# Splitting weights into high and low parts: the two parts side by side in one buffer, and moving tiles 288 floats apart

## The chip, the cores and the metric

One core of one Trainium2 chip runs the whole program. The metric is the device time of one execution in microseconds (us); for several executions the median is given. TensorE is called PE in the rows, its weight loads PEld; DVE is VectorE, ACT is ScalarE, POOL is GpSimd, SP is SyncE.

## What is computed

One inference step of a two-layer decoder trunk, on 256 prompt tokens and 8 sampled tokens at once (264 columns). Cut to what matters:

```python
for l in range(2):
    p = rmsnorm(h, norm1_g[l]) @ w_in[l]          # 2048 -> 5120
    a, bg, cg, hh, q, k, v, g, u, vv = split(p, 10)
    mix = concat(pool_mixer(a), conv_mixer(bg, cg, hh), retention(q, k, v, g), sgu_mixer(u, vv))
    h = h + mix @ w_out[l]                         # 2048 -> 2048
    gt, up = split(rmsnorm(h, norm2_g[l]) @ w_gate_up[l], 2)   # 2048 -> 2 x 5632
    h = h + (silu(gt) * up) @ w_down[l]            # 5632 -> 2048
y = rmsnorm(h, final_norm_g)
```

All inputs are float32 and the result has to be close to a float32 product. The mixers are small beside the four large products.

## The kernel before, in words

Activations lie transposed: 128 channels on the partitions, the 264 tokens along the free dimension. Every large product is made of 128x128 weight blocks. TensorE takes them in a reduced float32 form (`F32R`), so each operand is split in two: a high part, which is the value rounded to that form, and a low part, which is the remainder. A product of a weight block and a moving tile is then three matmuls into the same PSUM bank, in the function `work`:

```python
mm(ps, wl, xh[:], c["left"] == c["nk"], False)   # low weights,  high activations
mm(ps, wh, xl[:], False, False)                  # high weights, low activations
mm(ps, wh, xh[:], False, c["left"] == 0)         # high weights, high activations
```

Each of them is one weight load of 128 columns and one matmul with 264 moving columns; the weight load of the next matmul runs while the present one streams.

Weights come from HBM by DMA from SP's queue into `raw` (seven buffers, each of 8 blocks of 128x128, 512 KB). `do_split` (line 270 and the helper at line 120) turns a `raw` buffer into a high buffer `whi` with a cast on ScalarE and into a low buffer `wlo` with a subtraction on VectorE. There are four buffers of each kind (`NH = 4`). In them a block is 128 floats in a row per partition, and the high and the low buffer lie 16 KB apart. Weight buffers are split up to four ahead of the matmuls that read them, and loaded up to seven ahead of the split; waits between engines are semaphores. One buffer of 8 blocks feeds 24 matmuls.

The moving tiles are `XH[k]` and `XL[k]` (high and low part of the normalised input, 16 each) for the input and the gate/up product, and tiles `r` from a pool of 33 for the output and the down product. They lie next to each other, 264 floats (1,056 bytes) apart on each partition. Matmuls of the large products are written out in the rows as `acc<-xh,wlo`, `acc<-xl,whi`, `acc<-xh,whi`, `acc<-r,wlo` and `acc<-r,whi`. They all go through the helper `mm` at line 117. The small matmuls of the mixers go into `ms` banks, most of them in plain float32: such a matmul stands in the trace as two records.

Phases follow each other per layer: `in` (40 output chunks of 16 blocks), `out` (16 chunks of 16), then three groups of `gu` (32, 32 and 24 chunks of 16) and `dn` (16 chunks of 16, 16 and 12 blocks). In the `in` phase the generators in `tasks` (pooling, retention, gated unit) put their small matmuls between the chunks. For the retention of the sampled tokens, a constant `sel` of 8 blocks of 128 columns picks one token and spreads it over the partitions.

Of the kernel before, what the change touches and what calls it, by code (L numbers as in the profile page):

```python
# [11 lines left out]
F32R = mybir.dt.float32r  # L12
I32 = mybir.dt.int32
AF = mybir.ActivationFunctionType
ALU = mybir.AluOpType
AX = mybir.AxisListType

P = 128
L = 2
D = 2048  # L20
KD = D // P
NP = 256
NS = 8
T = NP + NS
# [8 lines left out]
SUB = 8  # L33
NH = 4
NR = 7
NT = 20
NRR = 33
TW = 272
TB = 88
VL = 32  # L40

# [10 lines left out]
def hybrid_step(ctx, tc, I, O):  # L52
    nc = tc.nc
    pe, ve, se, po, sy = nc.tensor, nc.vector, nc.scalar, nc.gpsimd, nc.sync
# [4 lines left out]
    def mk(name, shape, dt=F32):  # L59
        return sb.tile(shape, dt, tag=name, name=name)  # L60

    H4 = [mk(f"h{i}", [P, 4, T]) for i in range(4)]
    h = [H4[k // 4][:, k % 4, :] for k in range(KD)]
    XH = [mk(f"xh{k}", [P, T], F32R) for k in range(KD)]
    XL = [mk(f"xl{k}", [P, T], F32R) for k in range(KD)]
    raw = [mk(f"raw{i}", [P, SUB, P]) for i in range(NR)]
    whi = [mk(f"whi{i}", [P, SUB, P], F32R) for i in range(NH)]
    wlo = [mk(f"wlo{i}", [P, SUB, P], F32R) for i in range(NH)]
    rfree = deque(mk(f"r{i}", [P, T], F32R) for i in range(NRR))
    tfree = deque(mk(f"t{i}", [P, TW]) for i in range(NT))  # L70
    acc = [pp.tile([P, 512], F32, tag=f"acc{i}", name=f"acc{i}") for i in range(4)]
    misc = deque(pp.tile([P, 512], F32, tag=f"ms{i}", name=f"ms{i}") for i in range(4))
# [6 lines left out]
    ccol = mk("ccol", [P, 6 + 4 * 16 + KD])  # L79
    kdec, rcnt = ccol[:, 0:4], ccol[:, 6:70].rearrange("p (g t) -> p g t", g=4)  # L80
    mean128, mean2048, gfin = ccol[:, 4:5], ccol[:, 5:6], ccol[:, 70:70 + KD]
    sel = mk("sel", [VL + NS, NS, P], F32R)

    cols = mk("cols", [P, NC_COL])
    sgrow = mk("sgrow", [P, GW])
# [9 lines left out]
    vhl = mk("vhl", [VL + NS, GW], F32R)  # L95
# [8 lines left out]
    def ta():  # L104
        return tfree.popleft()

    def tf(*ts):
        tfree.extend(ts)

    def ma():  # L110
        return misc.popleft()

    def mf(*ts):
        misc.extend(ts)

    def mm(out, lhsT, rhs, start=True, stop=True):
        pe.matmul(out, lhsT, rhs, start=start, stop=stop)  # L117

    def tt(out, a, b, op, eng=None):
        (eng or ve).tensor_tensor(out=out, in0=a, in1=b, op=op)  # L120

    def stt(out, a, s, b, op0, op1):
        ve.scalar_tensor_tensor(out=out, in0=a, scalar=s, in1=b, op0=op0, op1=op1)  # L123

    def ts(out, a, s1, s2, op0, op1, eng=None):
        if s2 is None:
            (eng or ve).tensor_scalar(out=out, in0=a, scalar1=s1, scalar2=None, op0=op0)
        else:
            (eng or ve).tensor_scalar(out=out, in0=a, scalar1=s1, scalar2=s2, op0=op0, op1=op1)

    def scaled(out, a, s):
        se.activation(out, a, AF.Identity, scale=s)  # L132

    def f(ap):
        return ap.bitcast(F32)
# [8 lines left out]

    def split(src):
        hi, lo = rfree.popleft(), rfree.popleft()
        se.copy(hi[:], src)  # L147
        tt(lo[:], src, f(hi[:]), ALU.subtract)
        return hi, lo

    def split_ps(src, s):
        hi, lo = rfree.popleft(), rfree.popleft()
        scaled(hi[:], src, s)
        stt(lo[:], src, s, f(hi[:]), ALU.mult, ALU.subtract)
        return hi, lo

    def token_rsqrt(srcs, wcol):
        n = len(srcs)
        ps = ma()
        for c in range(3):  # L160
            cc = slice(c * TB, (c + 1) * TB)
            for i, parts in enumerate(srcs):
                for x, part in enumerate(parts):
                    mm(ps[:TB, c * n + i:c * n + i + 1], part[:, cc], wcol, x == 0, x == len(parts) - 1)
        w = 3 * n
        m, t, r = (small[:TB, q, :w] for q in range(3))
        ts(m, ps[:TB, :w], EPS, None, ALU.add, None)
        mf(ps)
# [3 lines left out]
    def token_bcast(ps, r, i, n):  # L172
        for c in range(3):
            mm(ps[:, c * TB:(c + 1) * TB], r[:, c * n + i:c * n + i + 1].to_broadcast([TB, P]), ident[:TB, :TB])

# [31 lines left out]
            return (r, ps) if both else r  # L207

    def to_x(k, gcol):
        scaled(XH[k][:], h[k], gcol)  # L210
        stt(XL[k][:], h[k], gcol, f(XH[k][:]), ALU.mult, ALU.subtract)

    subs = []
    phases = []
# [68 lines left out]
    def work(c, k0, k1, xs):  # L283
        if c["ps"] is None:
            c["ps"] = accfree.popleft()
        ps = c["ps"][:, :T]
        for k in range(k0, k1):
            j = c["subs"][k // SUB]
            if k == k0 or k % SUB == 0:
                do_split(j + NH)  # L290
                assert state["split"] > j
            wh, wl = whi[j % NH][:, k % SUB, :], wlo[j % NH][:, k % SUB, :]
            xh, xl = xs[k]
            mm(ps, wl, xh[:], c["left"] == c["nk"], False)
            mm(ps, wh, xl[:], False, False)
            c["left"] -= 1
            subs[j]["left"] -= 1
            mm(ps, wh, xh[:], False, c["left"] == 0)

    def run(cs, xs, evac, stats=None, bcast=None, hooks=None, defer=2):  # L300
        nk = cs[0]["nk"]
# [59 lines left out]
    def in_phase(l, cs, rms, hooks=None):  # L361
# [22 lines left out]
        def evac(c):  # L384
# [15 lines left out]
            elif grp == O_VV:  # L400
                vvT[j] = ta()
                tt(vvT[j][:, :T], ps[:, :T], r[:, :T], ALU.mult)
                if j == 0:
                    tasks.append(ret_sample())
# [50 lines left out]
        def pool(j, e):  # L455
            win = WINDOWS[j]
            s, w = e, 1
            while w < win:
                o = ta()
                lo = 2 * w - 1  # L460
                tt(o[:, lo:TW], s[:, lo:TW], s[:, lo - w:TW - w], ALU.add)
                if s is not e:
                    tf(s)
                s, w = o, 2 * w
            d, t = ta(), ta()
            stt(d[:, :NP], s[:, 16:TW], 1.0 / win, e[:, 16:TW], ALU.mult, ALU.subtract)
            tt(t[:, 0:16], s[:, 16:32], rcnt[:, j, :], ALU.mult)
            tt(d[:, 0:16], t[:, 0:16], e[:, 16:32], ALU.subtract)
            ve.tensor_reduce(out=t[:, 16:24], in_=exts[:, j, :, 16 - win:16], axis=AX.X, op=ALU.add)
            stt(d[:, NP:T], t[:, 16:24], 1.0 / win, exts[:, j, :, 15], ALU.mult, ALU.subtract)  # L470
            po.tensor_copy(pouts[:, j, :], e[:, TW - 15:TW])
            tf(s, e, t)
# [50 lines left out]
        def ret_sample():  # L523
            yield
            yield
            yield
            ob = None
            for b in range(NS + 1):
                if b > 0:
                    if ob is None:  # L530
                        ob = ma()
                    S = sst[(b - 1) % 3]
                    for j in range(4):
                        mm(ob[:, j * NS + b - 1:j * NS + b], S[:, j, :], qs[:, j, b - 1:b])
                    po.dma_start(out=O["ret_s"][l, :, b - 1], in_=S[:])
                    if b + 2 < NS:
                        sy.dma_start(out=S[:], in_=I["s_ret"][l, :, b + 2])
                if b < NS:
                    S = sst[b % 3]
                    vb = ma()  # L540
                    mm(vb[:], sel[:, b, :], vhl[:])
                    for j in range(4):
                        se.mul(S[:, j, :], S[:, j, :], GAMMA[j])
                        stt(S[:, j, :], vb[:, j * P:(j + 1) * P], ks[:, j, b:b + 1], S[:, j, :], ALU.mult, ALU.add)
                    mf(vb)
                yield
            for j in range(4):
                se.copy(oT[j][:, NP:T], ob[:, j * NS:(j + 1) * NS])
            mf(ob)
# [67 lines left out]

        run(cs, list(zip(XH, XL)), evac, rms.stats, bcast, hooks)
        assert not tasks
# [15 lines left out]
    def gu_phase(cs, rms, r2):  # L635
# [22 lines left out]
        if rms is None:  # L658
            run(cs, list(zip(XH, XL)), evac)
        else:  # L660
            run(cs, list(zip(XH, XL)), evac, rms.stats, bcast)
        return act, X["r"]
# [19 lines left out]
    with tc.manual_schedule():  # L682
        se.dma_start(out=cols[:], in_=I["cols"][0])
        state["load"] = state["split"] = 1
        src = subs[0]["src"]
# [48 lines left out]
        r, ps = rms.bcast(True)  # L734
# [9 lines left out]
def _constants():  # L744
    f4 = np.float32
    half = 64
    inv = (f4(10000.0) ** (-np.arange(half, dtype=f4) / f4(half))).astype(f4)
    pos = np.concatenate([np.arange(NP), np.full(NS, PAST)]).astype(f4)
    ang = (pos[:, None] * inv[None, :]).astype(f4).astype(np.float64)
    cos, sin = np.cos(ang).T, np.sin(ang).T  # L750
    c = np.concatenate([cos, cos], 0)
    s = np.concatenate([sin, -sin], 0)
    tabs = np.stack([c, s, c * RET_ROOT, s * RET_ROOT], 1).astype(f4)
    idx = np.arange(P, dtype=np.float64)
    lg = LG.astype(np.float64)
    diff = idx[None, :] - idx[:, None]
    maskt = np.where(diff[:, None, :] >= 0, np.exp(np.maximum(diff, 0.0)[:, None, :] * lg[None, :, None]), 0.0).astype(f4)
    qdec = np.broadcast_to(np.exp((idx + 1.0)[None, :] * lg[:, None])[None], (P, 4, P)).astype(f4)
    kdec = np.exp((P - 1.0 - idx)[:, None] * lg[None, :])
    rcnt = np.stack([1.0 / np.minimum(np.arange(16) + 1, w) for w in WINDOWS])  # L760
    eye = np.eye(P)
    sq128 = np.stack([eye, eye - 1.0 / P], 1).astype(f4)
    sel = np.zeros((VL + NS, NS, P), f4)
    sel[:NS] = sel[VL:] = np.eye(NS)[:, :, None]
    ccol = np.concatenate([kdec, np.full((P, 1), 1.0 / P), np.full((P, 1), 1.0 / D), np.broadcast_to(rcnt.reshape(1, 64), (P, 64))], 1).astype(f4)
    return dict(tabs=tabs, maskt=maskt, qdec=qdec, sq128=sq128, sel=sel), ccol

# [79 lines left out]
```

## Time and profile before

| | |
|---|---|
| time, median of 3 | 2299.62 us (2298.99 to 2299.68) |
| profiled execution, span of its instructions | 2298.7 us (no other time of this execution is given) |
| PE matmul busy | 2276.2 us, 99% |
| PE weight loads busy | 2263.9 us, 98% |
| DVE busy | 1350.1 us, 59% |
| ACT busy | 944.1 us, 41% |
| POOL busy | 289.4 us, 13% |
| DMA | 415.84 MB, mean 181 GB/s |

How to read it: the profile is of one execution. Records of matmuls overlap, since each one holds its filling and draining as well; so how fast the stream runs is read from how many matmuls start in a stretch, not from their mean duration. "The chain that ended last" follows the last instruction back to whatever released it.

### The profile page before, as it was taken

The numbers are of one execution on the slowest core, as the hardware profiler recorded it, in microseconds if no ns is written. First come the engines' busy times: TensorE is split into PE (matmuls) and PEld (weight loads), VectorE is DVE, ScalarE is ACT, GpSimd is POOL, SyncE is SP. The second block draws the span as 40 slices with busy tenths as digits, with TensorE's granted clock in tenths as the row PEclk, the third lists the DMA queues.
The fourth block names the chain that finished last, engine by engine and source line by source line (L and its number), as shares of the span: only waits on it lengthen the run. The fifth ranks groups of instructions, "written<-read, shape, count | busy, mean of one in ns | idle before, by whom it ended". The sixth has DMA issues, their size and how long they took to land.

```text
span 2298.7 us, 44403 instructions
## 1 busy us (share of the span) xinstructions
PE 2276.2 (99%) x18650; PEld 2263.9 (98%) x18650; DVE 1350.1 (59%) x1822; ACT 944.1 (41%) x1267; POOL 289.4 (13%) x404
## 2 busy tenths in 40 slices
PE   8999999999999999999999999999999999999997
PEld 7999999999999999999999999999999999999997
DVE  7558755555455555555665686655554555545554
ACT  5344344444334433343533433544443344333444
POOL 4112111111001110011121211111100111001111
PEclk9999999999999999999999999999999999999999
DMA  8565556656656656565655555556665566665653
GB/s 302 159 190 166 175 179 204 194 181 183 182 171 189 182 167 198 176 182 154 200 176 173 183 169 167 189 175 184 181 185 180 179 183 183 182 179 181 181 152 120
DMA packets 120314, 415.84 MB, mean 181 GB/s; under 512 B 14392, under 2 KB 14808, under 8 KB 120112
## 3 DMA queue, kind: packets, MB, share of 16 engines
q1 hardware_dynamic: 117792, 406.83, 58.1%
q0 software_dynamic: 2176, 6.13, 0.7%
q8 instruction: 146, 2.39, 0.4%
q14 instruction: 56, 0.46, 0.1%
q10 hardware_dynamic: 144, 0.03, 0.0%
HBM read 404.80 MB, written 8.13 MB: 180 GB/s over the span
## 4 chain that ended last, share of the span: by engine, by line
PE 99%; DVE 1%; issue 0%; DMA 0%; ACT 0%; SPq 0%; DVEq 0%; ACTq 0%
PE acc L117 95%; PE ms L117 3%; DMA h<-in_x 0%; DVE h L120 0%; DVE xl L123 0%; DVE wlo L120 0%; PE ms L587 0%; PE ms L490 0%; PE ms L491 0%; DVE small L123 0%; ACT whi L270 0%; ACT vhl L345 0%; ACT xh L132 0%; DVE small L120 0%; ACT t L187 0%
## 5 line engine op out<-in xcount | busy, mean ns | idle before, releaser
L120 DVE TENSOR_TENSOR wlo<-raw,whi 128x1024 fp32r<-128x1024 f32 (+1 forms) x769 | 978.0, 1279 | 658.7 <-ACT whi L270 652.6
L117 PE MATMUL acc<-xh,wlo 128*128 128x264 f32 x4096 | 1172.1, 286 | 8.9 <-DVE wlo L120 7.7
L117 PE MATMUL acc<-xl,whi 128*128 128x264 f32 x4096 | 1164.2, 284 | 0.2
L117 PE MATMUL acc<-xh,whi 128*128 128x264 f32 x4096 | 1162.2, 284 | 0.0
L270 ACT CAST whi<-raw 128x1024 fp32r<-128x1024 f32 (+1 forms) x767 | 781.9, 1029 | 613.8 <-PE acc L117 391.8
L117 PEld LDWEIGHTS acc<-xh,wlo 128*128 128x128 f32 x4096 | 773.8, 189 | 15.1 <-ACT xh L132 6.5
L117 PEld LDWEIGHTS acc<-xl,whi 128*128 128x128 f32 x4096 | 774.0, 189 | 1.9 <-DVE xl L123 1.4
L117 PEld LDWEIGHTS acc<-xh,whi 128*128 128x128 f32 x4096 | 770.4, 188 | 0.0
L117 PE MATMUL acc<-r,whi 128*128 128x264 f32 x3840 | 703.9, 284 | 0.0
L117 PEld LDWEIGHTS acc<-r,whi 128*128 128x128 f32 x3840 | 596.2, 188 | 0.0
L117 PE MATMUL acc<-r,wlo 128*128 128x264 f32 x1920 | 546.9, 285 | 0.0
L120 POOL TENSOR_TENSOR t<-t,t 128x264 f32<-128x264 f32 x281 | 220.4, 784 | 1749.7 <-ACT t L647 1245.2
L117 PEld LDWEIGHTS acc<-r,wlo 128*128 128x128 f32 x1920 | 361.2, 188 | 0.0
L120 DVE TENSOR_TENSOR t<-acc,t 128x264 f32<-128x264 f32 (+2 forms) x288 | 123.8, 430 | 112.4 <-PE acc L117 111.7
L147 ACT CAST r<-t 128x264 fp32r<-128x264 f32 x112 | 46.3, 413 | 292.9 <-DVE t L120 266.9
L647 ACT ACTIVATE t<-t 128x264 f32<-128x264 f32 x88 | 37.4, 425 | 190.8 <-DVE t L120 190.8
L120 DVE TENSOR_TENSOR h<-h,acc 128x264 f32<-128x264 f32 x128 | 54.5, 427 | 51.0 <-PE acc L117 50.7
L120 DVE TENSOR_TENSOR r<-t,r 128x264 fp32r<-128x264 f32 x112 | 48.5, 433 | 53.8 <-ACT r L147 53.8
L132 ACT ACTIVATE xh<-h,cols 128x264 fp32r<-128x264 f32 x64 | 31.7, 513 | 91.9 <-DVE h L120 91.8
L123 DVE SCALAR_TENSOR_TENSOR xl<-h,cols,xh 128x264 fp32r<-128x264 f32 x64 | 35.3, 565 | 28.1 <-ACT xh L132 28.1
L187 ACT ACTIVATE t<-h 128x264 f32<-128x264 f32 x74 | 29.9, 412 | 27.2 <-DVE h L120 27.2
L123 DVE SCALAR_TENSOR_TENSOR sst<-ms,ks,sst 128x128 f32<-128x128 f32 x64 | 18.0, 344 | 13.9 <-PE ms L117 9.2
(103 smaller groups left out, 405.6 us busy)
## 6 DMA issues: line engine op xcount, KB each, us to landing
raw<-in_w_gu SPq DMA_DIRECT2D x352, 512.0 KB, 4.2
raw<-in_w_dn SPq DMA_DIRECT2D x160, 512.0 KB, 3.7
raw<-in_w_in SPq DMA_DIRECT2D x159, 512.0 KB, 4.3
raw<-in_w_out SPq DMA_DIRECT2D x64, 512.0 KB, 4.4
raw<-in_w_dn SPq DMA_DIRECT2D x32, 256.0 KB, 3.5
sst<-in_s_ret SPq DMA_DIRECT2D x16, 256.0 KB, 4.3
out_ret_s<-sst POOLq DMA_DIRECT2D x16, 256.0 KB, 3.0
out_y<-h SPq DMA_DIRECT2D x7, 264.0 KB, 2.6
```

What stands on the lines that cost most here:

```text
L117: pe.matmul(out, lhsT, rhs, start=start, stop=stop)
L120: (eng or ve).tensor_tensor(out=out, in0=a, in1=b, op=op)
L123: ve.scalar_tensor_tensor(out=out, in0=a, scalar=s, in1=b, op0=op0, op1=op1)
L132: se.activation(out, a, AF.Identity, scale=s)
L147: se.copy(hi[:], src)
L187: se.activation(s[:, :T], src, AF.Square)
L270: se.copy(hi, src)
L647: se.activation(s[:, :T], t[:, :T], AF.Sigmoid)
```

## The change

High and low weights of a buffer go into one buffer `wsp` of shape [128, 8, 128, 2]: float 0 of a pair is the high part, float 1 the low part. `whi` and `wlo` become views of it with a step of two floats, and so do all that write or read them: the cast on ScalarE, the subtraction on VectorE (which reads the high part and writes the low one) and the weight loads on TensorE. The moving tiles keep their 264 columns, but each gets 288 floats (1,152 bytes) of room. To make space, `sel` keeps one column per token instead of 128 equal ones; the weight load reads that column with step zero. No instruction is added or removed, and on every engine the instructions and their waits stand in the same order as before.

```diff
+XW = 288
@@
-    XH = [mk(f"xh{k}", [P, T], F32R) for k in range(KD)]
-    XL = [mk(f"xl{k}", [P, T], F32R) for k in range(KD)]
+    XH = [mk(f"xh{k}", [P, XW], F32R)[:, :T] for k in range(KD)]
+    XL = [mk(f"xl{k}", [P, XW], F32R)[:, :T] for k in range(KD)]
     raw = [mk(f"raw{i}", [P, SUB, P]) for i in range(NR)]
-    whi = [mk(f"whi{i}", [P, SUB, P], F32R) for i in range(NH)]
-    wlo = [mk(f"wlo{i}", [P, SUB, P], F32R) for i in range(NH)]
-    rfree = deque(mk(f"r{i}", [P, T], F32R) for i in range(NRR))
+    wsp = [mk(f"wsp{i}", [P, SUB, P, 2], F32R) for i in range(NH)]
+    whi, wlo = ([w[:, :, :, q] for w in wsp] for q in range(2))
+    rfree = deque(mk(f"r{i}", [P, XW], F32R)[:, :T] for i in range(NRR))
@@
-    sel = mk("sel", [VL + NS, NS, P], F32R)
+    sel = mk("sel", [VL + NS, NS], F32R)
@@
-                    mm(vb[:], sel[:, b, :], vhl[:])
+                    mm(vb[:], sel[:, b:b + 1].to_broadcast([VL + NS, P]), vhl[:])
@@
-    sel = np.zeros((VL + NS, NS, P), f4)
-    sel[:NS] = sel[VL:] = np.eye(NS)[:, :, None]
+    sel = np.zeros((VL + NS, NS), f4)
+    sel[:NS] = sel[VL:] = np.eye(NS)
```

The rest of the diff drops `[:]` behind tiles that are now views.

## Rows read from the trace of the kernel before

**Rows 1.** The page: busy time of the engines with shares of the span and instruction counts, the granted clock in 40 slices (9 is 90% or more), and the chain that ended last by engine and by line.

```profile
PE 2276.2 (99%) x18650; PEld 2263.9 (98%) x18650; DVE 1350.1 (59%) x1822; ACT 944.1 (41%) x1267; POOL 289.4 (13%) x404
PEclk9999999999999999999999999999999999999999
PE 99%; DVE 1%; issue 0%; DMA 0%; ACT 0%; SPq 0%; DVEq 0%; ACTq 0%
PE acc L117 95%; PE ms L117 3%; DMA h<-in_x 0%; DVE h L120 0%; DVE xl L123 0%; DVE wlo L120 0%; PE ms L587 0%; PE ms L490 0%; PE ms L491 0%; DVE small L123 0%; ACT whi L270 0%; ACT vhl L345 0%; ACT xh L132 0%; DVE small L120 0%; ACT t L187 0%
```

**Rows 2.** The chain that ended last in order of time: start in us, length in us, what, and how many. These are the two longest pieces, nothing but large matmuls of the `out`, `gu` and `dn` phases of either layer.

```profile
391.65 763.19 PE acc L117 x6294
...
1524.48 758.80 PE acc L117 x6258
```

**Rows 3.** Groups of PE and PEld instructions by line, tiles and shape: partitions and columns of the weights (128*128), moving operand, count | busy us, mean ns of one | idle us before them and what ended it.

```profile
L117 PE MATMUL acc<-xh,wlo 128*128 128x264 f32 x4096 | 1172.1, 286 | 8.9 <-DVE wlo L120 7.7 <-DVE t L120 1.2
L117 PE MATMUL acc<-xl,whi 128*128 128x264 f32 x4096 | 1164.2, 284 | 0.2
L117 PE MATMUL acc<-xh,whi 128*128 128x264 f32 x4096 | 1162.2, 284 | 0.0
L117 PE MATMUL acc<-r,whi 128*128 128x264 f32 x3840 | 703.9, 284 | 0.0
L117 PE MATMUL acc<-r,wlo 128*128 128x264 f32 x1920 | 546.9, 285 | 0.0
...
L117 PEld LDWEIGHTS ms<-qs,sst 128*128 128x128 f32 x128 | 15.7, 191 | 0.0
...
L117 PEld LDWEIGHTS ms<-ccol,t 128*88 128x88 f32 x108 | 9.4, 157 | 1.0 <-ACT t L187 1.0
```

**Rows 4.** Matmuls of the gate/up product in order of time: start in us, length in us. The first seven rows and the last seven are the same places of two buffers of 8 blocks in succession, 24 matmuls apart.

```profile
1016.03 0.29 PE L117 MATMUL acc<-xh,wlo 128*128 128x264 f32 x1
1016.16 0.28 PE L117 MATMUL acc<-xl,whi 128*128 128x264 f32 x1
1016.28 0.28 PE L117 MATMUL acc<-xh,whi 128*128 128x264 f32 x1
1016.40 0.28 PE L117 MATMUL acc<-xh,wlo 128*128 128x264 f32 x1
1016.52 0.28 PE L117 MATMUL acc<-xl,whi 128*128 128x264 f32 x1
1016.63 0.28 PE L117 MATMUL acc<-xh,whi 128*128 128x264 f32 x1
1016.75 0.28 PE L117 MATMUL acc<-xh,wlo 128*128 128x264 f32 x1
...
1018.93 0.29 PE L117 MATMUL acc<-xh,wlo 128*128 128x264 f32 x1
1019.06 0.28 PE L117 MATMUL acc<-xl,whi 128*128 128x264 f32 x1
1019.18 0.28 PE L117 MATMUL acc<-xh,whi 128*128 128x264 f32 x1
1019.30 0.28 PE L117 MATMUL acc<-xh,wlo 128*128 128x264 f32 x1
1019.42 0.28 PE L117 MATMUL acc<-xl,whi 128*128 128x264 f32 x1
1019.53 0.28 PE L117 MATMUL acc<-xh,whi 128*128 128x264 f32 x1
1019.65 0.28 PE L117 MATMUL acc<-xh,wlo 128*128 128x264 f32 x1
```

**Rows 5.** Two places in the `in` phase where small matmuls follow each other, in order of time, as above (x8: eight instructions from the first start to the last end). First the weight loads and matmuls with one moving column, then four float32 matmuls with 128 moving columns.

```profile
135.24 0.98 PEld L117 LDWEIGHTS ms<-qs,sst 128*128 128x128 f32 x8
...
1333.37 0.61 PE L117 MATMUL ms<-sguw,vn 128*128 128x128 f32 x4
```

**Rows 6.** The mean length of one float32 matmul record with 128 moving columns, from the same view as rows 3.

```profile
L117 PE MATMUL ms<-sguw,vn 128*128 128x128 f32 x32 | 4.9, 274 | 0.0
```

**Rows 7.** Groups of DVE and ACT instructions by shape: the two splitting instructions of a buffer, and the small ones with and without a step. `zs` is written with a step of 3 floats, `exts` with a step of 16; the two rows with 16 floats write a tile without a step.

```profile
L120 DVE TENSOR_TENSOR wlo<-raw,whi 128x1024 fp32r<-128x1024 f32 x735 | 951.0, 1302 | 618.4 <-ACT whi L270 618.1
...
L120 DVE TENSOR_TENSOR t<-t,t 128x16 f32<-128x16 f32 x8 | 1.4, 175 | 0.3
...
L120 DVE TENSOR_TENSOR t<-t,ccol 128x16 f32<-128x16 f32 x8 | 1.4, 169 | 0.0
L120 DVE TENSOR_TENSOR zs<-acc,t 128x8 f32<-128x8 f32 x8 | 1.3, 158 | 0.0
L120 DVE TENSOR_TENSOR exts<-acc,t 128x8 f32<-128x8 f32 x8 | 1.3, 157 | 0.0
...
L270 ACT CAST whi<-raw 128x1024 fp32r<-128x1024 f32 x735 | 763.9, 1047 | 605.7 <-PE acc L117 383.7 <-issue 189.4 <-ACT whi L270 28.4
```

**Rows 8.** The page: the DMA queue that loads the weights, with its packets, MB and share of 16 engines' span; and the costliest groups of instructions, of which the two splitting lines with all their forms.

```profile
q1 hardware_dynamic: 117792, 406.83, 58.1%
...
L120 DVE TENSOR_TENSOR wlo<-raw,whi 128x1024 fp32r<-128x1024 f32 (+1 forms) x769 | 978.0, 1279 | 658.7 <-ACT whi L270 652.6
...
L270 ACT CAST whi<-raw 128x1024 fp32r<-128x1024 f32 (+1 forms) x767 | 781.9, 1029 | 613.8 <-PE acc L117 391.8
```

More of the change, by code (lines that the diff above doesn't have):

```diff
@@ L146, in split @@
         hi, lo = rfree.popleft(), rfree.popleft()
-        se.copy(hi[:], src)
-        tt(lo[:], src, f(hi[:]), ALU.subtract)
+        se.copy(hi, src)
+        tt(lo, src, f(hi), ALU.subtract)
         return hi, lo
@@ L152, in split_ps @@
         hi, lo = rfree.popleft(), rfree.popleft()
-        scaled(hi[:], src, s)
-        stt(lo[:], src, s, f(hi[:]), ALU.mult, ALU.subtract)
+        scaled(hi, src, s)
+        stt(lo, src, s, f(hi), ALU.mult, ALU.subtract)
         return hi, lo
@@ L209, in to_x @@
     def to_x(k, gcol):
-        scaled(XH[k][:], h[k], gcol)
-        stt(XL[k][:], h[k], gcol, f(XH[k][:]), ALU.mult, ALU.subtract)
+        scaled(XH[k], h[k], gcol)
+        stt(XL[k], h[k], gcol, f(XH[k]), ALU.mult, ALU.subtract)
     subs = []
@@ L293, in work @@
             xh, xl = xs[k]
-            mm(ps, wl, xh[:], c["left"] == c["nk"], False)
-            mm(ps, wh, xl[:], False, False)
+            mm(ps, wl, xh, c["left"] == c["nk"], False)
+            mm(ps, wh, xl, False, False)
             c["left"] -= 1
             subs[j]["left"] -= 1
-            mm(ps, wh, xh[:], False, c["left"] == 0)
+            mm(ps, wh, xh, False, c["left"] == 0)
     def run(cs, xs, evac, stats=None, bcast=None, hooks=None, defer=2):
```

## The prediction

> **What bounds the kernel now.** The page comes first. It shows TensorE's matmuls busy for 99% of the span, VectorE for 59% and ScalarE for 41%, the granted clock at its upper level in every slice, and a chain that ended last of which 95% is the large matmuls at line 117 [rows 1]. Then the same chain in order of time: 6,294 matmuls in 763.19 us and 6,258 in 758.80 us with nothing between them [rows 2], so 121.3 ns from one start to the next. In the groups, the first of the three kinds of matmul waited 8.9 us in all and the others next to nothing [rows 3]. The large matmuls number 3 x 4,096 + 3,840 + 1,920 = 18,048 [rows 3]; at 121.3 ns they make 2,189 us, which is the 95%. So one number decides: the pitch of a pair of weight load and matmul. One nanosecond of it is worth 18.0 us.
>
> Is 121.3 ns the least that this pair can take? Two short places say no. Eight weight loads with only one moving column to compete take 0.98 us from the first start to the last end; with 191 ns for the last [rows 3], seven steps take 0.79 us, 113 ns each [rows 5]. Four float32 matmul records with 128 moving columns take 0.61 us; with 274 ns for the last [rows 6], three steps take 112 ns each, although each has a full weight load beside it [rows 5]. The main stream is 8 to 9 ns above these.
>
> Where is the excess? The timeline shows that it hangs on the place. From 1016.03 the steps are 0.13, 0.12, 0.12, 0.12, 0.11, 0.12 us, and 24 matmuls later, from 1018.93, the same six again [rows 4]. What repeats after 24 matmuls is which addresses the moving tile and the weights have: eight blocks later the weights lie in another buffer at the same places within it, and moving tiles spaced 1,056 bytes have moved by 33 x 256 bytes. I read this as the moving stream and the weight load, which read the same memory at the same time, now and then wanting the same part of it.
>
> Their speeds fit. A load takes (191 - 157)/(128 - 88) = 0.85 ns per float [rows 3], so it walks 4.7 bytes per ns. The moving stream walks 1,056 bytes in at most 121.3 ns, so 8.7 bytes per ns or more, about twice as fast: it overtakes the load again and again. In the float32 records with 128 columns both walk 512 bytes in a step, at the same speed, and there the excess is gone [rows 5].
>
> **The change, part by part.** No instruction comes, goes or moves, and no wait is added. What changes is addresses.
>
> *Weight load with a step of two floats.* It covers 1,024 bytes in its 109 ns (128 x 0.85), 9.4 bytes per ns: about the speed of the moving stream. Then the two keep their distance; at worst they meet once per pair and go on shifted. No row shows a load with a step. Its bounds: below, the pitch cannot fall under the 112 to 113 ns of rows 5; above, if each stepped float cost two, a load would take 218 ns and the pitch with it. I take the rate per float unchanged, since these rows are the nearest, and 2 ns above the floor for a meeting per pair, because the float32 records that walk in step read only half as many bytes per ns as the main stream would: 115 ns.
>
> *Moving tiles 1,152 bytes apart.* All now start at a multiple of 128 bytes from each other, and so do the blocks of weights (1,024 bytes), so every pair begins with one of two distances. That keeps the result even over the blocks; I count it with the first part.
>
> *Cast and subtraction with a step.* Each buffer costs ScalarE 1.05 us and VectorE 1.30 us [rows 7], and the matmuls of a buffer last 24 x 115 ns = 2.76 us. Small stepped writes show no price: 8 floats written with a step of 3 or 16 take 158 and 157 ns, 16 floats without one 169 and 175 ns [rows 7]. I take nothing. What hides them is VectorE's spare time: all else on it is 1,350.1 - 978.0 = 372 us [rows 1, 8], so in a run of 2,185 us the 769 subtractions would bind only from (2,185 - 372)/769 = 2.36 us each, 1.8 times today's mean of 1.28 us. ScalarE has more room: it waited 391.8 us for the matmuls to free a buffer [rows 8]. Were it to double, VectorE would need 769 x 2.56 + 372 = 2,341 us and bind; that end lies beyond the range, among the slower cases.
>
> The Trainium skill has a rule here ("SBUF — State Buffer", section "Door 1: The DMA port swizzle"): memory is read in lines of 16 bytes, and full speed wants at least two hits on a line. A step of two floats gives exactly two hits, so by it neither the loads nor the two splitting instructions get slower, but each load crosses 64 lines instead of 32. No row of before shows a two-float step of any length.
>
> *DMA.* 406.83 MB take 58.1% of the engines' time [rows 8]; in a span 5% shorter that is 61%. Hidden. `sel` with a step of zero concerns 16 small matmuls: nothing.
>
> **Sum.** 18,048 x (121.3 - 115) ns = 113.7 us. 2,298.7 - 113.7 = 2,185.0 us for the profiled span; the median of the runs lies 0.9 us above that span, so 2,186 us.
>
> **Rivals.**
>
> *Only a part of the excess goes.* If the two streams still drift (the speeds 8.7 and 9.4 are bounds, not equal), meetings become fewer, not rare. For it: nothing shows the moving stream in step at its full speed. Pitch 118 to 120.9, taken as 119.5: 18,048 x 1.8 = 32 us less, 2,267 us.
>
> *The change does nothing.* The excess would come from something else within the pair, such as handing over from load to matmul, and the repeating pattern from the order of instructions, which also repeats after 24. Against it: the order is the same for each block, three matmuls long, and the steps within the 24 still differ [rows 4]. 2,299.6 us. The Trainium skill states a rule that amounts to this ("TensorE: Matmul & The Clock Gate", section "Step-by-step: what each phase is for"): matmul and weight load have independent read ports, and a load takes no read bandwidth from the running matmul. The trace doesn't bear it out as far as rows 4 reach.
>
> *Slower: the load meets the stream twice as often.* A stepped load touches twice as many addresses. If meetings are counted by addresses touched and the distance doesn't hold, the excess of 121.3 - 113 = 8.3 ns doubles: 18,048 x 8.3 = 150 us more, 2,449 us. Or they stay in step at the wrong distance and meet all the time, which is worse. It decides from the point where a stepped load adds over 0.25 ns to the pitch (4.6 us, 0.2%). For it: rows 5 show walking in step only for a slower stream.
>
> **Chances.** About 0.2% (4.6 us) is what a measurement of this kernel can tell from no change. Walking in step, 0.55; a part, 0.17; so faster 0.72. No change 0.06. Slower 0.22, most of it far off. The likeliest has its own range from the pitch: 112 ns gives 2,132, 113 ns gives 2,150, 118 ns gives 2,240 us. The whole range goes from 2,140, between the two floors, to 2,310 us: it takes in the partial case, no change and slightly slower, and leaves out the slower cases by more, some 0.18, with the bound of a load at half speed.
>
> **What would show it.** In the profile after: the chain's long pieces, 6,294 and 6,258 matmuls, at about 724 and 720 us (115 ns each); steps in the timeline equal within 0.01 us, without the 0.13; weight loads at 188 to 191 ns as now; the splitting rows at 1.05 and 1.30 us; PE's waits for `wlo` still some 10 us. It is wrong if the long pieces grow (loads meet more), if the weight load's mean goes up (a step has a price), or if PE's idle time before `acc<-xh,wlo` runs to tens of us (VectorE has become the bound).

## The result and the profile after

| | before | after |
|---|---|---|
| time, median of 4 | 2299.4 us | 2316.93 us (2316.55 to 2317.87) |
| ratio | | 1.0076, 95% interval 1.0063 to 1.0089 |
| span of the profiled execution | 2298.7 us | 2314.8 us |

The kernel is 17.5 us slower, 0.76%. The forecast was 2,186 us.

The page of after: busy time by engine, and the splitting cast on ScalarE, which now writes with a step. They answer to [rows 1] and [rows 8].

```profile
PE 2293.1 (99%) x18650; PEld 2280.8 (99%) x18650; DVE 1341.7 (58%) x1822; ACT 1009.4 (44%) x1267; POOL 290.2 (13%) x404
...
L121 DVE TENSOR_TENSOR wsp<-raw,wsp 128x1024 fp32r<-128x1024 f32 (+1 forms) x769 | 969.8, 1269 | 699.4 <-ACT wsp L271 687.6
...
L271 ACT CAST wsp<-raw 128x1024 fp32r<-128x1024 f32 (+1 forms) x767 | 847.3, 1116 | 583.8 <-PE acc L118 372.9
```

The chain that ended last, in order of time; the same two pieces as in [rows 2].

```profile
391.95 769.35 PE acc L118 x6294
...
1533.95 765.02 PE acc L118 x6258
```

Matmuls and weight loads by shape, which answer to [rows 3].

```profile
L118 PE MATMUL acc<-xh,wsp 128*128 128x264 f32 x8192 | 1525.7, 286 | 8.3 <-DVE wsp L121 7.1 <-DVE t L121 1.2
...
L118 PEld LDWEIGHTS acc<-xh,wsp 128*128 128x128 f32 x8192 | 1319.4, 197 | 14.4 <-ACT xh L133 6.6 <-issue 4.8 <-DVE t L121 1.6
L118 PEld LDWEIGHTS acc<-xl,wsp 128*128 128x128 f32 x4096 | 803.4, 196 | 1.8 <-DVE xl L124 1.4
L118 PEld LDWEIGHTS acc<-r,wsp 128*128 128x128 f32 x5760 | 705.0, 197 | 0.0
```

The two long pieces grew by 6.16 and 6.22 us, with the same counts. Over their 12,552 matmuls the pitch went from 121.25 to 122.24 ns; 0.99 ns x 18,048 = 17.8 us, which is the whole loss. TensorE waits no more than before (8.3 us against 8.9), VectorE's subtraction is no dearer, and the cast, 87 ns longer in the mean, stays hidden: ScalarE still waits 372.9 us for buffers. What is new on TensorE is the weight load: 188 to 189 ns before, 196 to 197 now. Two of its rows of before, the slowest and the fastest of the large ones:

```profile
L117 PEld LDWEIGHTS acc<-xl,whi 128*128 128x128 f32 x4096 | 774.0, 189 | 1.9 <-DVE xl L123 1.4
...
L117 PEld LDWEIGHTS acc<-r,whi 128*128 128x128 f32 x3840 | 596.2, 188 | 0.0
```

The steps have not become equal. In the long pieces they ran from 115 to 131 ns before and run from 117 to 130 now, by the starts in the traces. In the timeline of after the step behind a matmul of `xl` is now 0.13 us, now 0.12 (x2: two matmuls):

```profile
1024.19 0.29 PE L118 MATMUL acc<-xl,wsp 128*128 128x264 f32 x1
1024.32 0.40 PE L118 MATMUL acc<-xh,wsp 128*128 128x264 f32 x2
1024.56 0.28 PE L118 MATMUL acc<-xl,wsp 128*128 128x264 f32 x1
1024.68 0.41 PE L118 MATMUL acc<-xh,wsp 128*128 128x264 f32 x2
```

### The profile page after: what moved, and what is told of

Read it like the earlier page. It is cut to its first block, busy times and chain, and to the rows that moved or that the text cites. A ratio compares the mean times of both kernels' runs of the same rounds, so it can differ in the third digit from the quotient of the medians.

```text
span 2314.8 us, 44403 instructions
## 1 busy us (share of the span) xinstructions
PE 2293.1 (99%) x18650; PEld 2280.8 (99%) x18650; DVE 1341.7 (58%) x1822; ACT 1009.4 (44%) x1267; POOL 290.2 (13%) x404
## 3 DMA queue, kind: packets, MB, share of 16 engines
q1 hardware_dynamic: 117792, 406.83, 57.4%
## 4 chain that ended last, share of the span: by engine, by line
PE 99%; DVE 1%; issue 0%; DMA 0%; ACT 0%; SPq 0%; DVEq 0%; ACTq 0%
PE acc L118 95%; PE ms L118 3%; DVE xl L124 0%; DVE h L121 0%; DMA h<-in_x 0%; DVE wsp L121 0%; PE ms L588 0%; PE ms L492 0%; PE ms L491 0%; ACT wsp L271 0%; DVE small L124 0%; ACT vhl L346 0%; ACT xh L133 0%; DVE small L121 0%; DVE t L121 0%
## 5 line engine op out<-in xcount | busy, mean ns | idle before, releaser
L118 PE MATMUL acc<-xh,wsp 128*128 128x264 f32 x8192 | 1525.7, 286 | 8.3 <-DVE wsp L121 7.1
L121 DVE TENSOR_TENSOR wsp<-raw,wsp 128x1024 fp32r<-128x1024 f32 (+1 forms) x769 | 969.8, 1269 | 699.4 <-ACT wsp L271 687.6
L118 PEld LDWEIGHTS acc<-xh,wsp 128*128 128x128 f32 x8192 | 1319.4, 197 | 14.4 <-ACT xh L133 6.6
L118 PE MATMUL acc<-xl,wsp 128*128 128x264 f32 x4096 | 1177.7, 288 | 0.2
L271 ACT CAST wsp<-raw 128x1024 fp32r<-128x1024 f32 (+1 forms) x767 | 847.3, 1116 | 583.8 <-PE acc L118 372.9
L118 PEld LDWEIGHTS acc<-xl,wsp 128*128 128x128 f32 x4096 | 803.4, 196 | 1.8 <-DVE xl L124 1.4
L118 PE MATMUL acc<-r,wsp 128*128 128x264 f32 x5760 | 705.7, 285 | 0.0
L118 PEld LDWEIGHTS acc<-r,wsp 128*128 128x128 f32 x5760 | 705.0, 197 | 0.0
L118 PE MATMUL ms<-t,t 128*128 128x128 f32 x112 | 17.7, 274 | 0.0
L118 PEld LDWEIGHTS ms<-qs,sst 128*128 128x128 f32 x128 | 15.7, 191 | 0.0
```

The costliest lines, as they stand in the source:

```text
L271: se.copy(hi, src)
```

## The experiments

### Each half of the change alone

`move288` keeps the tiles 288 floats apart and takes the pairing back; `pairs264` does the reverse.

```diff
 move288, against the changed kernel
-    wsp = [mk(f"wsp{i}", [P, SUB, P, 2], F32R) for i in range(NH)]
-    whi, wlo = ([w[:, :, :, q] for w in wsp] for q in range(2))
+    whi = [mk(f"whi{i}", [P, SUB, P], F32R) for i in range(NH)]
+    wlo = [mk(f"wlo{i}", [P, SUB, P], F32R) for i in range(NH)]
 pairs264, against the changed kernel
-XW = 288
+XW = 264
```

> Only the moving tiles are 288 floats apart; high and low weights lie in buffers of their own without a step, as before (sel has one column per token, as in the changed kernel). If the stepped load is what costs the time, this one is not slower than before, and faster if the even distances help: pitch 119 to 121 ns, 2258 to 2295 us. If the distance of the moving tiles is what costs, it is as slow as the changed kernel, 2310 to 2320 us. If the pitch hardly depends on addresses, it stays within 0.3% of 2299 us.

> Only the weights are interleaved; the moving tiles stay 264 floats apart. If the stepped load costs, this one is as slow as the changed kernel or slower, 2310 to 2340 us, with the weight loads' mean at 196 to 197 ns as there. If the distance of the moving tiles costs, it is at 2299 us or faster, although the loads' mean has grown.

`move288` took 2307.20 us, a ratio of 1.0033 (1.0021 to 1.0045): 7.6 us slower. `pairs264` took 2328.49 us, 1.0126 (1.0112 to 1.0139): 28.9 us slower. Both halves lose, the step more; together they lose 17.5 us, less than the step alone. So neither half of the idea gains by itself, but with the step the room of 288 floats gives back some 11 us.

### TensorE alone

The next kernels run little else than pairs of load and matmul, so that each cost stands apart. An operand "walks" when each float is read from a new place; with step zero it "stands", and one column is read again and again. The pitch is the mean time from one start to the next. The core of the first, `pairs_alone`, cut to what matters:

```python
STAGES = (  # name, step of weights, room of a moving tile, columns, order
    ("wa", 1, 264, 264, "kernel"), ("wb", 2, 288, 264, "kernel"),
    ("wc", 1, 288, 264, "kernel"), ("wd", 2, 264, 264, "kernel"),
    ("we", 1, 264, 264, "fixed"),  ("wf", 0, 264, 264, "fixed"),
    ("wg", 1, 0, 264, "fixed"),    ("wh", 0, 0, 264, "fixed"),
...
for i, (w, m) in enumerate(seq):
    pe.matmul(ps, w, m, start=i == 0, stop=i == len(seq) - 1)
```

> Leaves out the whole step: 14 stages of 192 pairs of weight load and matmul each, on TensorE alone, and zeros for most outputs. Stages wa to wd take the blocks and tiles in the kernel's order: wa as before, wb as changed, wc only the tiles 288 apart, wd only the step. If the pitch is TensorE's own matter, wa takes 121 ns per pair and wb 122; if other engines disturb it, both are lower by several ns. we to wh repeat one pair: we with a fixed tile and a fixed block, wf with a weight column read with step zero, wg with a moving column read with step zero, wh with both. If meetings in memory make the excess over 113 ns, wh is at 112 to 113 and we above it; if the excess is something else in the pair, all four are alike at 120 to 122. wi and wj have 232 and 192 moving columns: a pitch that falls by 0.4 ns per column is set by the stream, one that stays by the load. wk, wl and wm have 64 columns, so the load alone decides, with a step of 1, 2 and 4 floats: equal if a step has no price, 112 against 220 ns if a stepped float costs two. wn has 512 columns: about 0.42 ns per column if the stream decides.

Its first stages in order of time: the first matmul of `wa`, `wb`, `wc`, `wd` and `we`, each stage 192 pairs long.

```profile
21.36 0.28 PE L142 MATMUL acc<-xha,waq 128*128 128x264 f32 x1
...
44.56 0.29 PE L142 MATMUL acc<-xhb,wb 128*128 128x264 f32 x1
...
68.03 0.28 PE L142 MATMUL acc<-xhb,wcq 128*128 128x264 f32 x1
...
91.40 0.29 PE L142 MATMUL acc<-xha,wd 128*128 128x264 f32 x1
...
114.97 0.53 PE L142 MATMUL acc<-xha,we 128*128 128x264 f32 x3
```

23.20, 23.47, 23.37 and 23.57 us over 192 pairs are 120.8 ns as before, 122.2 as changed, 121.7 with the tiles alone moved and 122.8 with the step alone. The kernels stand in the same order. The distances from before are larger here, by 0.3 to 0.5 ns: 0.9, 1.4 and 1.9 ns, against 0.4, 1.0 and 1.6 in `move288`, the changed kernel and `pairs264` (the differences of their times over 18,048 pairs). The splitting and the mixers are gone; ScalarE had 6.9 us of casts left in the first stage and next to nothing after it, and DMA still ran during the first two. So the loss is made between load and stream on TensorE itself.

Now the stages that repeat one pair (x192). Busy time less the last one's mean, over 191, is the pitch to within 0.3 ns; the figures given below are counted from the starts in the trace:

```profile
L142 PE MATMUL acc<-xha,we 128*128 128x264 f32 x192 | 23.5, 283 | 0.0
...
L142 PE MATMUL acc<-xha,wf 128*128 128x264 f32 x192 | 23.2, 282 | 0.0
...
L142 PE MATMUL acc<-xha,wh 128*128 128x264 f32 x192 | 22.3, 277 | 0.0
L142 PE MATMUL acc<-xha,wg 128*128 128x264 f32 x192 | 22.3, 277 | 0.0
...
L142 PE MATMUL acc<-xha,wi 128*128 128x232 f32 x192 | 21.6, 275 | 0.0
L142 PE MATMUL acc<-xha,wj 128*128 128x192 f32 x192 | 21.6, 274 | 0.0
```

A load that does not walk through memory (`wf`) brings the pitch from 121.3 to 120.0 ns only. A moving column that does not walk (`wg`, `wh`) brings it to 115.2, whether the load walks or not. With 232 or 192 columns it is 111.6 to 111.7 and no longer depends on them: there the load binds. The last four stages cannot be set beside these, because the granted clock fell (last section). Among themselves they can: at a granted clock of 0.50 a pair with 64 columns took 213 ns with a step of one float (`wk`), the same 213 with two (`wl`) and 233 with four (`wm`). So at that level the step of two had no price. `wn` (512 columns) took 233 ns after the clock was back at 1.00.

### How many columns, and how many of the load

> Leaves out the whole step: 19 stages of 144 repeated pairs on TensorE alone. wa to wk: fixed block without a step, fixed tile, 192, 224, 240, 248, 256, 264, 288, 320, 384, 448 and 512 columns. wl to wn: the same with a moving column read with step zero, 264, 320 and 512 columns. wo, wp, wq: a load with a step of 2, 4 and 8 floats beside 192 columns; wr: step zero beside 192. ws and wt (512 columns): load with step zero and with step 2; wu: load without a step, moving tile with a step of 2 floats. If the stream's own reading sets the pitch, it is flat at 112 ns up to about 248 columns, then rises by 0.45 ns per column to about 233 at 512, and by 0.42 where the moving column doesn't walk; ws and wt are then like wk. If meetings with the load make the excess, the excess stays near 8 ns however many columns there are, so 512 columns take about 221 ns, and ws takes 215. If a stepped load has a price of its own, wo is above wa by 1 to 10 ns and wp and wq by more; if not, all are 112.

> Leaves out the whole step: 16 stages of 192 repeated pairs on TensorE alone. wa: 264 columns beside a full load, the reference of 120.0 ns. wb and wc: 232 columns of which none walks (step zero), beside a load with a step of 1 and of 2 floats; wd to wg: 232 walking columns, load with step 1, then with step 2 and the moving tile 0, 64 and 128 bytes behind it. If the step has a price of the load's own, wc is above wb by about the 7 ns that 192 columns showed; if the price comes from meeting the moving stream, wc is like wb (112) and only we to wg are above wd. wh, wi, wj: 264 walking columns beside a load of only 96, 64 and 32 columns; wk: 32-column load, moving column not walking; wl, wm, wn: 512 columns, with a full load, a load of 32 columns, and of 32 with the moving column not walking. If the excess of walking over not walking (120.0 against 115.2) comes from meeting the load, it shrinks with the load's columns and wj is near 115 to 116; if the moving stream alone makes it, wj stays at 120. wo and wp: a step of 3 floats, beside a moving column that doesn't walk and one that does.

From `columns`, fixed block and tile (x144): 512 columns walking (`wk`) and not (`wn`), 320 walking (`wh`) and not (`wm`), 264 with a step of 2 floats in the moving tile (`wu`), and 264, 256, 248 and 240 without.

```profile
L123 PE MATMUL acc<-wide,wu 128*128 128x264 f32 x144 | 34.7, 420 | 0.0
...
L123 PE MATMUL acc<-wide,wk 128*128 128x512 f32 x144 | 32.8, 389 | 0.0
L123 PE MATMUL acc<-wide,wn 128*128 128x512 f32 x144 | 31.6, 381 | 0.0
...
L123 PE MATMUL acc<-wide,wh 128*128 128x320 f32 x144 | 21.3, 309 | 0.0
L123 PE MATMUL acc<-wide,wm 128*128 128x320 f32 x144 | 20.1, 301 | 0.0
...
L123 PE MATMUL acc<-wide,wf 128*128 128x264 f32 x144 | 17.4, 281 | 0.0
L123 PE MATMUL acc<-wide,we 128*128 128x256 f32 x144 | 17.4, 283 | 0.0
...
L123 PE MATMUL acc<-wide,wd 128*128 128x248 f32 x144 | 16.5, 274 | 0.0
...
L123 PE MATMUL acc<-wide,wc 128*128 128x240 f32 x144 | 16.2, 274 | 0.0
```

The pitch is 111 to 112 ns up to 240 columns, 113.4 at 248, and 120 at 256 and 264: the stream takes over between them. At 320 columns it is 146.6 walking and 138.7 not, at 512 it is 227.0 and 218.7. Half of the expectation held (load below, stream above); the smooth rise of 0.45 ns per column did not. Beside 192 columns, where the load binds, the step of two (`wo`) took 118.6 ns against 111.5 without (`wa`): the first sign that it has a price. The step of four (`wp`) took 235 ns over its first 25 pairs, while the clock was at 1.00; the rest of it, `wq` and part of `wr` ran at the lower clock. `ws` and `wt` (512 columns, load with step zero and two) came out at 232 and 233 ns, above `wk`, which neither expectation had.

From `loads` (x192), with the clock at 1.000 throughout: `wb` to `we` have 232 columns, not walking with a load of step 1 and 2, walking with step 1 and 2; `wp` has step 3. `wa`, `wj` and `wk` have 264 columns: walking beside a full load, walking beside a load of 32 columns, and not walking beside one of 32.

```profile
L118 PE MATMUL acc<-wide,wp 128*128 128x232 f32 x192 | 33.5, 336 | 0.0
...
L118 PE MATMUL acc<-wide,wj 128*32 128x264 f32 x192 | 23.2, 282 | 0.0
L118 PE MATMUL acc<-wide,wa 128*128 128x264 f32 x192 | 23.2, 281 | 0.0
...
L118 PE MATMUL acc<-wide,we 128*128 128x232 f32 x192 | 22.8, 280 | 0.0
L118 PE MATMUL acc<-wide,wc 128*128 128x232 f32 x192 | 22.8, 281 | 0.0
...
L118 PEld LDWEIGHTS acc<-wide,wc 128*128 128x128 f32 x192 | 22.7, 196 | 0.0
...
L118 PE MATMUL acc<-wide,wk 128*32 128x264 f32 x192 | 22.3, 277 | 0.0
L118 PE MATMUL acc<-wide,wd 128*128 128x232 f32 x192 | 21.6, 275 | 0.0
L118 PE MATMUL acc<-wide,wb 128*128 128x232 f32 x192 | 21.6, 275 | 0.0
...
L118 PEld LDWEIGHTS acc<-wide,wb 128*128 128x128 f32 x192 | 21.5, 192 | 0.0
```

Two things are settled here. First, the step has a price of the load's own: 111.6 to 111.7 ns without, 117.8 with two floats, 173 with three, and the same whether the moving columns walk or stand still (only with the moving tile 128 bytes further, `wg`, it was 118.9). Second, the stream of 264 walking columns takes 120.0 ns beside a full load and 120.0 beside one a quarter as long (`wa`, `wj`; `wk`, standing, 115.2). What it takes beyond the 115.2 of a standing column is not made by the load. The second was measured at a start of 0 bytes alone, one of the cheapest in the next section. At 512 columns the stream took 226.9 ns beside a full load and 231.7 beside the short one, which nothing here explains.

### Where the tiles start

> Leaves out the whole step: 16 stages of 192 repeated pairs of 264 columns, load without a step; the moving tile starts 0, 16, 32 and so on to 240 bytes behind a multiple of 256, where the block starts. If streams meet in memory, the pitch goes up and down with the place, from 116 to 126 ns, with the same shape again after 128 or 256 bytes. If the moving stream alone makes the excess, all stages lie within 1 ns of 121.

> As place1, with a load that steps by two floats. If walking in step removes meetings except at some places, most stages are near 113 to 116 ns and a few high. If the step makes every stage dearer by a fixed price, the stages have the shape of place1 plus 1 to 2 ns. If the place matters more with the step, the spread between stages is wider than in place1, and the starts of the changed kernel (0 and 128 bytes) are among the lower ones.

> Leaves out the whole step: 26 stages of 144 pairs on TensorE alone, 264 walking columns, load without a step. In wa to wp each tile starts 0, 16, 32 and so on to 240 bytes behind the start of the one before it (modulo 256); wq, wr, ws the same by 8, 24 and 4 bytes; the last seven give three shifts in turn, in the order of the kernel's three matmuls: wt 128, 128, 0; wu 0, 0, 32 (the kernel before); wv 0, 0, 128 (the tiles 288 apart); ww 192, 64, 32; wx 64, 192, 32; wy 128, 128, 32; wz 128, 128, 64. If what counts is where a tile starts against the one before it, the stages differ by up to 8 ns, some near 115 to 117, and wu is below wv as the kernel before is below the one with tiles 288 apart. If it is the place alone, all are an average over their places, 121 to 122 ns, but for wa at 120.

In `place1`, seven of 16 starts gave 120.0 to 120.1 ns and the others up to 123.3 (the start at 128 bytes, `wi`); none was below 120. In `place2`, with the step, two starts kept 120.1 and the others lay up to 126.7 (the start at 64 bytes, `we`): the step made the mean 1.3 ns dearer, from 121.0 to 122.3, and the spread wider. Of the two starts of the changed kernel, 0 bytes (`wa`) took 120.1 and 128 bytes 122.2. The extreme stages and the same starts in the other run, `place1` first:

```profile
L118 PE MATMUL acc<-wide,wi 128*128 128x264 f32 x192 | 23.8, 287 | 0.0
...
L118 PE MATMUL acc<-wide,we 128*128 128x264 f32 x192 | 23.4, 283 | 0.0
...
L118 PE MATMUL acc<-wide,wa 128*128 128x264 f32 x192 | 23.2, 281 | 0.0
```

```profile
L118 PE MATMUL acc<-wide,we 128*128 128x264 f32 x192 | 24.5, 289 | 0.0
...
L118 PE MATMUL acc<-wide,wi 128*128 128x264 f32 x192 | 23.6, 285 | 0.0
...
L118 PE MATMUL acc<-wide,wa 128*128 128x264 f32 x192 | 23.2, 283 | 0.0
```

So what the step costs hangs on the place: 5.7 ns at 64 bytes (121.0 to 126.7), nothing at 0, and a gain of 1.1 ns at 128 bytes. The moving tile is the same in both runs and only the load differs, so at such places the load does slow the stream, although with a shorter stream beside it the stepped load takes 117.8 ns, less than these 121.0.

In `shifts` 26 ways of moving the start from one matmul to the next gave 120.0 to 122.8 ns and nothing near 115. The kernel's order before (`wu`) began at 371.91 us and `wv`, the tiles 288 apart, at 389.32, ended at 406.83: 120.9 against 121.6 ns over 144 pairs, the direction of `move288`, where the kernel lost 0.4 ns per pair.

### The places in the kernel

The cheap starts of `place1` (0, 192, 224 bytes), and as a control the dear ones (96, 128, 160), by room after every third tile:

```diff
-    XH = [mk(f"xh{k}", [P, T], F32R) for k in range(KD)]
-    XL = [mk(f"xl{k}", [P, T], F32R) for k in range(KD)]
+    X = row([f"xh{k}" for k in range(KD)] + [f"xl{k}" for k in range(KD)], (0, 0, 40))
+    XH, XL = X[:KD], X[KD:]
+    mk("roomraw", [P, 24])                 # in the control only
@@
-    rfree = deque(mk(f"r{i}", [P, T], F32R) for i in range(NRR))
+    mk("roomr", [P, 40])                   # in the control only
+    rfree = deque(row([f"r{i}" for i in range(NRR)], (40, 0, 0)))
```

> The kernel before with nothing changed but room of 160 bytes after every third moving tile, so that every tile starts 0, 192 or 224 bytes behind a multiple of 256 counted from the blocks of weights; loads without a step. The three places took 120.0 ns each in place1, the eight places of the kernel before 121.3 on average. If places in memory add up as the repeated pairs show, this is 1.3 x 18,048 = 23 us faster than before, 2276 us. If the order of different tiles matters as much as the place, it is anywhere from 2280 to 2310 us.

> The same rooms with the whole set shifted, so that every tile starts 96, 128 or 160 bytes behind: 121.64, 123.35 and 121.67 ns in place1, 122.2 on average. By the places it takes 0.9 x 18,048 = 16 us more than before, 2316 us, and 40 us more than the kernel with the cheap places. If the place does not carry over to the kernel, both are within 0.3% of each other.

`places` took 2300.30 us, 1.0006 (0.9997 to 1.0015): no gain where 23 us were expected. `places_dear` took 2317.68 us, 1.0080 (1.0066 to 1.0094), as expected. So a bad set of starts costs as much as the whole change did, but the good starts of repeated pairs don't carry over to a kernel in which tiles alternate. The kernel before, at 121.25 ns, is already within 1.3 ns of the 120.0 that no start undercut; no layout tried here beats it.

The control shows one thing more. The two rooms that it has beyond `places`, 24 and 40 floats, make 256 bytes together, so modulo 256 the moving tiles begin at the same places in both kernels. What has moved against them is `raw` and the blocks of weights, by 96 bytes. That alone cost 17.4 us, 0.96 ns per pair, with the cast on ScalarE at 1,047 ns in both. Where the load reads, beside the same moving tiles, changes the pitch by about 1 ns.

### The step on a third and on two thirds of the loads

`low_step` puts the low parts of two buffers side by side and leaves the high parts alone; `high_step` is the mirror image. The tiles stay where they were before.

```diff
-    wlo = [mk(f"wlo{i}", [P, SUB, P], F32R) for i in range(NH)]
+    wlp = [mk(f"wlp{i}", [P, SUB, P, 2], F32R) for i in range(NH // 2)]
+    wlo = [wlp[i // 2][:, :, :, i % 2] for i in range(NH)]
```

> The kernel before with only the low weights read with a step of two floats: the low parts of two buffers share one tile, float by float; high parts and moving tiles as before. A third of the large loads (6,016 of 18,048) have the step. If each stepped load has a price, this costs a third of what pairs264 cost (28.9 us): 9.6 us, 2308 us. If the price came from high and low lying side by side, or from the splitting instructions, it is 0 or near the whole.

> The mirror image: only the high weights, two thirds of the large loads (12,032), are read with the step. By a price per load 19.3 us, 2318 us; low_step and this one then add up to pairs264.

`low_step` took 2307.96 us, 1.0038 (1.0025 to 1.0052); `high_step` 2315.80 us, 1.0071 (1.0059 to 1.0084). Against the 2299.58 us of before that were measured with them, that is 8.4 and 16.2 us: 1.4 ns for each of 6,016 stepped loads, 1.35 for each of 12,032. In `low_step` only the low loads are longer:

```profile
L118 PEld LDWEIGHTS acc<-xh,wlp 128*128 128x128 f32 x4096 | 803.7, 196 | 14.0 <-ACT xh L133 6.0 <-issue 5.5 <-DVE wlp L121 1.2
...
L118 PEld LDWEIGHTS acc<-xh,whi 128*128 128x128 f32 x4096 | 773.0, 189 | 0.0
```

Its cast, which writes no step there, took 1,047 ns as before; in `high_step` it took 1,136:

```profile
L271 ACT CAST whi<-raw 128x1024 fp32r<-128x1024 f32 x735 | 763.9, 1047 | 609.0 <-PE acc L118 377.2 <-issue 198.8 <-ACT whi L271 23.3
...
L271 ACT CAST whp<-raw 128x1024 fp32r<-128x1024 f32 x735 | 828.5, 1136 | 575.0 <-PE acc L118 365.5 <-ACT whp L271 159.4 <-issue 42.3
```

So the price follows the loads, not the splitting instructions. Both together make 24.6 of the 28.9 us of `pairs264`; the rest is not explained.

## Why the prediction was wrong, point by point

**What bounds the kernel** was right: large matmuls one after another, 18 us for each nanosecond of pitch. The loss came out of just that product.

**"Is 121.3 ns the least that this pair can take? Two short places say no."** This is where it began to fail. The 113 and 112 ns of [rows 5] are the load's own rate beside short streams, 111.6 ns in `wb` of `loads`. At 264 columns the stream is the longer of the two and takes 115.2 ns even when it reads one column over and over, 120.0 when it walks. Only 1.3 ns of the 8 to 9 could have been won by any start tried here, and rows with one or 128 columns could not show that.

**"I read this as the moving stream and the weight load ... now and then wanting the same part of it."** This is the step that failed. The repeating 0.13 and 0.11 us of [rows 4] are real, and starts do matter (`places_dear` lost 18.9 us by them alone). Load and stream do get in each other's way, but plain loads by some 1 ns of the pitch: 1.3 ns from `we` to `wf` in `pairs_alone`, and the 0.96 ns between `places` and `places_dear` fit that. The bulk of the excess does not come from meeting: the pitch stays at 120.0 ns beside a load a quarter as long. Walking at the same speed therefore had next to nothing to remove. In the sum, 18,048 x (121.3 - 115) ns stood for a gain of 6.3 ns per pair; measured was a loss of 0.99. The sign that the prediction named, steps equal within 0.01 us, did not come either: they run from 117 to 130 ns, and the 0.13 us is still there. That the float32 records of [rows 5] showed no excess has a simpler reason that fits their 112 ns: with 128 columns beside a full load, the load binds.

**"I take the rate per float unchanged"** was wrong too. The step costs the load 6 ns, from 111.7 to 117.8; that lies within the bounds that the prediction gave, but it chose the end with no price. The Trainium skill's rule ("SBUF — State Buffer", section "Door 1: The DMA port swizzle") wants two hits on a line for full speed, and adds that each access which crosses to a new line pays a penalty; the prediction counted the 64 lines instead of 32 but gave them no price. The load measured 6% longer at two floats (two hits) and 55% longer at three (fewer than two), and the moving tile twice as long at two, so two hits were not full speed for either, and the measurement decides. Of the load's 6 ns only 1.35 to 1.6 reach the kernel's pitch, since the load lies beside a stream of 120 ns. Why as much as that arrives, when 117.8 is still below 120, stays open. Single steps of the stream that are shorter than the load are not enough: in the long pieces of before 4.8% of the steps were below 118 ns, and raising each of these to 117.8 would add 0.08 ns. And at 64 bytes no step in `place1` was shorter than 119 ns, yet there the stepped load added 5.7 ns.

**Moving tiles 288 floats apart: "That keeps the result even over the blocks."** Alone it cost 7.6 us in the kernel, 0.4 ns per pair, and 0.7 to 0.9 ns in the order of the kernel's pairs alone (121.6 to 121.7 against 120.8 to 120.9 ns). That it helps once the loads step, by 11 us, holds on TensorE alone as well (122.2 against 122.8 ns); its cause stays open.

**The parts counted as nothing** held: no instruction moved, TensorE's waits stayed at 8.3 us, the cast's 87 ns and the DMA were hidden. Small stepped writes on VectorE [rows 7] were a fair guide for VectorE (1,279 ns before, 1,269 after), not for ScalarE (1,029 and 1,116).

**The rivals.** "Slower: the load meets the stream twice as often" had the sign, and `place2` at 64 bytes shows something of the kind, but it had 150 us instead of 17.5. The Trainium skill's rule that load and matmul have independent read ports ("TensorE: Matmul & The Clock Gate", section "Step-by-step: what each phase is for") was set aside on the strength of rows 4; `wa` and `wj` agree with it at 120.0 ns each, at a start of 0 bytes. At 64 bytes the runs do not: with the same moving tile, the load's step alone took the pitch from 121.0 to 126.7. Even so the rule would have led closer to the truth than the reading of one timeline, since it leaves no large excess to be won.

## What to carry to other kernels

A floor must be taken from a place with the same operands: a pair of load and matmul is bound in the main by the longer of the two, and which one that is changed here between 240 and 256 moving columns. The shorter one can still add 1 to 2 ns, by where and how it reads. Before changing a layout for the sake of a pattern in a timeline, run the pair by itself and vary one side; a quarter of the load and a standing moving column would have answered it. Keep float32 weights contiguous: at the full clock a step of two floats made each load 6% longer, three 55%, and four more than doubled it (235 ns).

## What the runs showed of the hardware that was not expected

A moving tile with a step of two floats took 240 ns for 264 columns (`wu`), twice the contiguous one, while a load with such a step lost only 6%.

A stream of walking columns takes 5 to 8 ns more than one that reads a single column: 4.8 ns at 264 columns (120.0 against 115.2), 8.0 at 320 (146.6 against 138.7) and 8.3 at 512 (227.0 against 218.7). From 320 to 512 columns it hardly grows, so it is not a lower rate per column. At 512 columns other pairs took up to 233 ns. Repeated at the same start, it took the same 120 ns for 256 and for 264 columns. What makes this cost stays open.

The granted clock fell to half while pairs followed each other without a gap, in the stages of `pairs_alone` with 64 columns. Busy time by engine (x instructions), granted clock and DMA in four stretches: 192 columns, the change to 64, and twice 64:

```profile
227.00:248.00 21.00, 21.00 (x191) 21.00 (x190) 0.00 (x0) 0.35 (x1) 0.00 (x0) 1.00 0.01 2
248.00:255.00 7.00, 7.00 (x50) 7.00 (x48) 0.00 (x0) 0.32 (x1) 0.00 (x0) 0.73 0.00 0
260.00:280.00 20.00, 20.00 (x95) 20.00 (x96) 0.00 (x0) 0.00 (x0) 0.00 (x0) 0.50 0.00 1
300.00:320.00 20.00, 20.00 (x96) 20.00 (x95) 0.00 (x0) 0.00 (x0) 0.00 (x0) 0.50 0.00 0
```

With 192 columns it stayed at 1.00, the 2.4 GHz level; with 64 it went to 0.50, the 1.2 GHz level, although TensorE was busy throughout both.
